# Gate matrices of two prompt tiles by indirect accumulating DMAs, and the output projection in the expert weight buffers

## The chip, the cores and the metric

One core of one Trainium2 chip runs the whole layer. The metric is device microseconds of that core, from launch to end; the median of three runs of the kernel before is 2303.07 us (2301.51 to 2303.24).

## What is computed

The reference is one hybrid encoder layer on two token sets with shared weights: 512 prompt tokens (tiles 0 to 3 of 128) and 256 sample tokens (tiles 4 and 5). Attention comes first; the change touches the output projection behind it and the PEER layer:

```python
x = x + jnp.concatenate([o_a, o_b], axis=-1) @ w_out[l]
x = x + peer(rms_norm(x, ffn_norm_g[l]), ...)

def peer(h, w_q, sub_keys, u, v):          # per chunk of 128 tokens
    q = (xc @ w_q).reshape(TOKEN_CHUNK, PEER_HEADS, 2, D_KEY_HALF)
    sc = einsum('cpzk,znk->cpzn', q, sub_keys)
    top_v, top_i = lax.top_k(sc, PEER_TOPK)
    cand = top_v[:, :, 0, :, None] + top_v[:, :, 1, None, :]
    best, pos = lax.top_k(cand, PEER_TOPK)
    eidx = take_along_axis(cand_idx, pos)   # i * 128 + j
    g = softmax(best)
    act = gelu(einsum('cd,cpkd->cpk', xc, u[eidx]))
    return einsum('cpk,cpkd->cd', g * act, v[eidx])
```

There are 128 x 128 experts (i, j). Each token picks 8 heads x 16 = 128 of them, each with a gate weight.

## The kernel before, in words

All matrix products in float32 are made of three products of a high and a low part (`mm3`, `split`). The work stands in this order:

- The sample tokens are normalized and projected by `w_in` (`in_project`, weights `wraw` by SyncE's DMA queue, three buffers); sample attention, the prompt's projection, prompt attention and the sample's output projection follow and overlap.
- The sample tiles are routed (`route_keys`, `route_pairs`); `eidx` holds their experts.
- The prompt's output projection (L534 to L561): `mixed` splits the mixed heads into `mh` and `ml`, the weights `wraw` come through a pool of its own (`wout`, three buffers of 128x512), then four norm-transposes make `x2p`.
- Prompt routing (`route_keys` with `prompt_weights`) with the first 16 steps of `hidden`. `hidden(j)` (L589) loads the 512 KB block `uT[j]` into `raw`, splits it, multiplies it by all 512 prompt tokens in PSUM tile `pu` (24 matmuls), applies GELU and stores `h_d`. `weights8` gives it three `raw` buffers and two each of `hi` and `lo`.
- The gate stage (L630 to L657). For each prompt tile `picked` takes the chosen pairs and gate weights. Then VectorE makes one-hot matrices `oij` and the gate-weighted `og`, four tokens at a time TensorE multiplies them into `pg` (12 matmuls of 128 columns), ScalarE copies `pg` into `gb`, and 16 DMAs store `gb` to `g_d`, a dense gate matrix [i, j, token]. The remaining 112 steps of `hidden` are interleaved with it.
- The value stage (L680 to L702): 64 pairs of j. Gates `gblk` come from `g_d` (one load for 8 values of j), `gw` is the pair's activations from `h_d`, VectorE multiplies them (L688), the product is split into `w`, the values `raw` into `hi` and `lo`, and TensorE adds 48 matmuls into the eight `py` banks.
- Beside the prompt, the 256 sample tokens are done sparsely: 256 indirect gathers (`row`, L725, 1 MB each, issued by GpSimd into four buffers), each followed by a dot product (L727) and an accumulation `acc` (L735) on VectorE.

What sets the order: each engine runs its instructions in the order in which a scheduler wrote them when the program was built; `tc.add_manual_dep` with `NOSYNC` ties a dot product to a step of `hidden` or of the value stage (`early`, `low_of`) in that order without a wait. Each queue of DMAs is issued in order by its engine: loads and most stores by SyncE, `h_d` and `g_d` by ScalarE, indirect ones by GpSimd.

Of the kernel before, what the change touches and what calls it, by code (L numbers as in the profile page):

```python
# [11 lines left out]
F32 = mybir.dt.float32  # L12
F32R = mybir.dt.float32r
# [31 lines left out]
NCAND = 64  # L45
FIRST_GATHER = 36
FILL = 16
NOSYNC = mybir.DependencyInfo(mybir.DependencyClass.NoSync, mybir.DependencyReason.DATA)


@with_exitstack
def tile_kernel(ctx, tc, xs_in, relb, onehot, logm, g1, w_in, gqk, lamv, gdiff, w_out, g2,
# [7 lines left out]
    def pool(stack, name, bufs=1, side="left", **kw):  # L60
        return stack.enter_context(tc.tile_pool(name=name, bufs=bufs, side=side, reuse_waits="tile", **kw))
# [38 lines left out]
    g_d = dram.tile([DENSE * P // TB, P, NK, TB], F32, name="g_d")  # L100


    ident = const.tile([P, P], F32, name="ident")
# [6 lines left out]
    def stage():  # L110
        return late.tile([P, D], F32, tag="st4", name="st4", bufs=3)
# [50 lines left out]

        project(lhs, n, w_in, 6, banks, evac, lows)

    def attention(n, pj, hrs, mix, order, psc, ptr):
        w = n * P
        turn, turn2 = itertools.count(), itertools.count()

# [181 lines left out]
    attention(2, pjS, hrS, mixS, ORDER, [ps_sc], [ps_tr])  # L350
# [190 lines left out]
    wo = pool(wox, "wo", DC)  # L541
    half = []
    for d in range(DC):
        raw = wpool.tile([P, 512], F32, name="wraw")
        nc.sync.dma_start(raw, w_out[d * P:(d + 1) * P, 512:])
        wh = wo.tile([P, 512], F32R, name="woh")
        wl = wo.tile([P, 512], F32R, name="wol")
        split(wh, wl, raw, G if d % 2 else V)
        half.append((wh, wl))
# [80 lines left out]
    nxt = picked(0)  # L630
    for t in range(DENSE):
        ijT, gp_ = nxt
        if t + 1 < DENSE:
            nxt = picked(t + 1)
        for tb in range(P // TB):
            gb = gm.tile([P, NK, TB], F32, name="gb")
            for tq in range(TB // TQ):
                c0 = tb * TB + tq * TQ
                oij = gm.tile([P, 2, TQ, NK], BF, name="oij")
                og = [gm.tile([P, TQ, NK], BF, name=f"og{k}") for k in range(3)]  # L640
                both = [P, 2 * TQ, NK // 2, 2]
# [15 lines left out]
            nc.scalar.dma_start(g_d[t * (P // TB) + tb], gb)  # L657
# [10 lines left out]
    vrows = uv.rearrange("(i j) d -> j i d", j=NK)  # L668

    def gates(jb):  # L670
        gblk = dp.tile([P, DENSE * P // TB, JB, TB], F32, name="gblk")
        nc.sync.dma_start(gblk, g_d[:, :, jb * JB:(jb + 1) * JB, :].rearrange("b i j t -> i b j t"))
        return gblk

    def values_of(j):
        vr, vh, vl = weights8(vrows[j, :, D:].rearrange("i (c d) -> i c d", d=P))
# [3 lines left out]
    for jp in range(NK // 2):  # L680
        jj = 2 * jp % JB
        wh, wl = (late.tile([P, 2, 2, 512], F32R, tag=f"x{i}", name=f"w{i}") for i in range(2)) if jp == 0 else (wh, wl)
        if jj == 0:
            gblk = gates(2 * jp // JB)
        ge = dp.tile([P, 2, 512], F32, name="gw", bufs=3)
        nc.sync.dma_start(ge, h_d[jp])
        ge4 = ge.rearrange("p k (b t) -> p k b t", t=TB)
        V.tensor_tensor(ge4, ge4, gblk[:, :, jj:jj + 2].rearrange("p b k t -> p k b t"), op=OP.mult)  # L688
        gh, gl = wh[:, jp % 2], wl[:, jp % 2]
        split(gh, gl, ge, V)  # L690
        vv = [values_of(2 * jp + k) for k in range(2)]
# [101 lines left out]
```

## Time and profile before

| what | value |
| --- | --- |
| median of 3 runs | 2303.07 us |
| profiled execution, its own time | 2314.86 us |
| its span, first to last instruction | 2313.0 us |
| granted TensorE clock, mean | 0.969 |
| TensorE busy | 93% of the span |
| VectorE busy | 77% |
| ScalarE busy | 40% |
| GpSimd busy | 36% |
| moved by DMA | 617.65 MB |

The profile is one execution. Busy time of TensorE counts pipelined matmuls, so a full engine can show less than 100%. A wait is put down to what came last. A stretch of the span is named by its start and end in us.

### The profile page before, as it was taken

Reading aid. Unit: us, or ns where it says so; the run is one execution under the profiler, and the core shown is the slowest. Engines: PE = TensorE matmul, PEld = TensorE weight load, DVE = VectorE, ACT = ScalarE, POOL = GpSimd, SP = SyncE. Lnnn points to the kernel's source line nnn. Section 1 sums busy time; section 2 is a strip of 40 time slices with the busy share of each in tenths; the row PEclk is TensorE's granted clock in tenths of the full one; section 3 lists DMA queues with packets and bytes.
Section 4 is the critical chain, followed back from the end, with each engine's and each line's share of the span. In section 5 each row is a group of like instructions: output and inputs, shape, how many; then the busy total and the mean of one; then the engine's idle time right before and its main releaser. Section 6 shows DMA issues by size and latency. Waiting matters only on the chain.

```text
span 2313.0 us, 31093 instructions
## 1 busy us (share of the span) xinstructions
PE 2159.4 (93%) x11312; PEld 1779.3 (77%) x11312; DVE 1791.0 (77%) x3500; ACT 915.4 (40%) x1484; POOL 835.9 (36%) x634
## 2 busy tenths in 40 slices
PE   7999999848899989999999996999999999999998
PEld 4788789836687867877888875887887887888776
DVE  4645379992589899989999974676887887887886
ACT  4765577621322324554555532222222222223232
POOL 4767766623456532222223231221222222221221
PEclk9999999958899999999999998999999999999999
DMA  5633333303577776888998999898999899999985
GB/s 183 184 109 125 104 120 94 114 19 102 196 248 269 262 263 220 289 302 316 344 349 341 347 363 343 307 351 302 346 360 374 326 366 357 370 362 349 375 341 190
DMA packets 198681, 617.65 MB, mean 267 GB/s; under 512 B 16016, under 2 KB 82192, under 8 KB 163712
## 3 DMA queue, kind: packets, MB, share of 16 engines
q1 hardware_dynamic: 139968, 278.70, 34.8%
q0 software_dynamic: 36864, 268.45, 30.7%
q10 hardware_dynamic: 21696, 68.53, 7.7%
q8 instruction: 88, 1.44, 0.2%
q14 instruction: 65, 0.53, 0.1%
HBM read 542.17 MB, written 73.45 MB: 266 GB/s over the span
## 4 chain that ended last, share of the span: by engine, by line
PE 64%; DMA 12%; DVE 10%; issue 8%; POOL 4%; ACT 2%; SPq 0%; ACTq 0%; POOLq 0%; DVEq 0%
PE py L67 8%; PE py L68 8%; PE py L69 8%; PE pu L67 6%; PE pu L69 6%; PE pu L68 6%; DMA raw<-in_uv_dram 4%; PE pacc L68 3%; DMA row<-in_uv_dram,eidx 3%; PE pacc L69 3%; PE pacc L67 3%; POOL row L725 2%; DMA wraw<-in_w_in_dram 2%; PE pg L653 2%; PE pq L69 2%
## 5 line engine op out<-in xcount | busy, mean ns | idle before, releaser
L725 POOL DMA_INDIRECT row<-in_uv_dram,eidx x256 | 399.0, 1559 | 1179.3 <-DVE acc L735 1041.8
L72 ACT CAST hi<-raw 128x1024 fp32r<-128x1024 f32 x272 | 285.1, 1052 | 594.2 <-PE pu L68 237.4
L67 PE MATMUL pu<-x2p,hi 128*128 128x512 f32 x1024 | 409.5, 400 | 18.5 <-ACT hi L72 18.5
L69 PE MATMUL pu<-x2p,lo 128*128 128x512 f32 x1024 | 408.6, 400 | 15.7 <-DVE lo L73 11.8
L67 PE MATMUL py<-w,hi 128*128 128x512 f32 x1024 | 400.9, 393 | 18.4 <-ACT hi L72 15.9
L68 PE MATMUL pu<-x2p,hi 128*128 128x512 f32 x1024 | 406.6, 397 | 0.0
L73 DVE TENSOR_TENSOR lo<-raw,hi 128x1024 fp32r<-128x1024 f32 x236 | 287.4, 1221 | 151.6 <-ACT hi L72 123.3
L68 PE MATMUL py<-w,hi 128*128 128x512 f32 x1024 | 400.4, 391 | 1.1 <-DVE w L73 1.1
L727 DVE CUSTOM_DVE_ANT_0 row<-row,st 128x1024 f32<-128x1024 f32 x256 | 332.2, 1305 | 64.0 <-DMA row<-in_uv_dram,eidx 63.9
L735 DVE SCALAR_TENSOR_TENSOR acc<-row,wgt,acc 128x1024 f32<-128x1024 f32 x256 | 328.2, 1282 | 5.3
L69 PE MATMUL py<-w,lo 128*128 128x512 f32 x1024 | 294.2, 389 | 0.4 <-DVE lo L73 0.4
L67 PEld LDWEIGHTS py<-w,hi 128*128 128x128 f32 x1024 | 193.2, 189 | 66.1 <-ACT hi L72 23.6
L67 PEld LDWEIGHTS pu<-x2p,hi 128*128 128x128 f32 x1024 | 195.5, 191 | 61.7 <-ACT hi L72 20.2
L69 PEld LDWEIGHTS pu<-x2p,lo 128*128 128x128 f32 x1024 | 194.9, 190 | 59.5 <-DVE lo L73 16.1
L68 PEld LDWEIGHTS py<-w,hi 128*128 128x128 f32 x1024 | 193.4, 189 | 41.4 <-DVE w L73 1.6
L68 PEld LDWEIGHTS pu<-x2p,hi 128*128 128x128 f32 x1024 | 195.0, 190 | 38.8
L69 PEld LDWEIGHTS py<-w,lo 128*128 128x128 f32 x1024 | 192.1, 188 | 40.7 <-DVE lo L73 0.8
L656 ACT COPY gb<-pg 128x512 f32<-128x512 f32 x128 | 132.5, 1142 | 82.1 <-PE pg L653 81.1
L73 POOL TENSOR_TENSOR wl<-wraw,wh 128x512 fp32r<-128x512 f32 x96 | 126.0, 1319 | 86.3 <-ACT wh L72 82.3
L72 ACT CAST w<-gw 128x1024 fp32r<-128x1024 f32 x64 | 67.0, 1049 | 168.4 <-PE py L69 167.7
L72 ACT CAST wh<-wraw 128x512 fp32r<-128x512 f32 x120 | 74.4, 623 | 104.0 <-DMA wraw<-in_w_in_dram 38.7
L732 ACT ACTIVATE wgt<-h 128x2 f32<-128x2 f32 x128 | 26.2, 205 | 224.8 <-DVE h L727 223.0
(303 smaller groups left out, 3700.5 us busy)
## 6 DMA issues: line engine op xcount, KB each, us to landing
raw<-in_uT_dram SPq DMA_DIRECT2D x128, 512.0 KB
raw<-in_uv_dram SPq DMA_DIRECT2D x128, 512.0 KB
h_d<-ge ACTq DMA_DIRECT2D x128, 256.0 KB
g_d<-gb ACTq DMA_DIRECT2D x16, 2048.0 KB
gblk<-g_d SPq DMA_DIRECT2D x16, 2048.0 KB
gw<-h_d SPq DMA_DIRECT2D x64, 512.0 KB
wraw<-in_w_in_dram SPq DMA_DIRECT2D x96, 256.0 KB
toe<-bias_d SPq DMA_DIRECT2D x24, 448.0 KB
```

The lines of the kernel that those rows point to most:

```text
L67: T.matmul(ps, ah, bh, start=start, stop=False)
L68: T.matmul(ps, ah, bl, start=False, stop=False)
L69: T.matmul(ps, al, bh, start=False, stop=stop)
L72: S.copy(hi, raw)
L73: return (low or G).tensor_tensor(lo, raw, f(hi), op=OP.subtract)
L653: T.matmul(pg[:, c], oij[:, 0, c4 * 4 + c], og[k][:, c4 * 4 + c], start=k == 0, stop=k == 2)
L656: S.copy(gb[:, :, o:o + 4].rearrange("p j t -> p t j"), pg)
L725: G.indirect_dma_start(out=r, out_offset=None, in_=uv, in_offset=bass.IndirectOffsetOnAxis(ap=eidx[t][:, b + k:b + k + 1], axis=0))
L727: dot = V.tensor_tensor_reduce(r[:, :D], r[:, :D], x2r[t], 1.0, 0.0, OP.mult, OP.add, h[:, k:k + 1])
L732: S.activation(wgt, h, AF.Gelu)
L735: V.scalar_tensor_tensor(acc, rows[k][:, D:], wgt[:, k:k + 1], acc, op0=OP.mult, op1=OP.add)
```

## The change

1. `SCAT = 2`: the gate matrices of prompt tiles 0 and 1 are no longer made by one-hot products. Two arrays `s_d` [i, j, token] of 8 MB each in DRAM are filled with zeros by 16 DMAs of 1 MB (`clear`, written into the sample attention, one pair behind each A head). For each tile the index `si` = (i * 128 + j) * 128 + token and the gate weight `gt` are made on VectorE, and 128 indirect DMAs per tile (`put`), each of 128 single floats, add the weights into `s_d`. `NOSYNC` ties put `k` to `hidden` step 24 + k * 92 / 256. Tiles 2 and 3 stay as they were; `g_d` halves.
2. The value stage loads `gs` from `s_d` beside a half-sized `gblk`, and multiplies `gw` in two halves.
3. The prompt's output projection loads `w_out` in blocks of 512 KB through `raw8`, `hi8` and `lo8` of the expert weights, and the pool `wout` is gone.

```diff
+    s_d = [dram.tile([P, NK, P], F32, name=f"s_d{t}") for t in range(SCAT)]
...
+    zero = stage()
+    V.memset(zero, 0.0)
+
+    def clear(kind, h):
+        if kind == 0:
+            for s_ in s_d:
+                nc.sync.dma_start(s_.rearrange("i j t -> i (j t)")[:, h * 2048:(h + 1) * 2048]
+                                  .rearrange("i (a n) -> i a n", n=D), zero[:, None].to_broadcast([P, 2, D]))
+
+    attention(2, pjS, hrS, mixS, ORDER, [ps_sc], [ps_tr], clear)
...
-    project((mh, ml), 4, w_out, 1, (obanks,), evac)
+    def out_weights(d, nb, hi, lo):
+        raw = wide(rw.tile([P, DC, P], F32, name="raw8", bufs=3))
+        nc.sync.dma_start(raw, w_out[d * P:(d + 2) * P, nb * 512:(nb + 1) * 512].rearrange("(k p) n -> p k n", p=P))
+        split(hi, lo, raw, G if d % 4 else V)
+        return hi, lo
...
+    for t in range(SCAT):
+        gt, si = (o[t][:, 0].rearrange("p k h -> p (k h)") for o in (tv, ti))
+        ei, ej = route_pairs(rq, t, gt)
...
+        V.tensor_scalar(i_, i_, float(P), tok, op0=OP.mult, op1=OP.add)
+        V.tensor_copy(si, i_)
+        scat.append((si, gt))
+    nxt = picked(SCAT)
+    for t in range(SCAT, DENSE):
...
+    for k in range(NPK * SCAT):
+        t, c = k % SCAT, k // SCAT
+        si, gt = scat[t]
+        put = G.indirect_dma_start(out=s_d[t].rearrange("i j (t one) -> (i j t) one", one=1),
+                                   out_offset=bass.IndirectOffsetOnAxis(ap=si[:, c:c + 1], axis=0),
+                                   in_=gt[:, c:c + 1], in_offset=None, compute_op=OP.add)
+        after = low_of[FIRST_SCATTER + k * (LAST_SCATTER - FIRST_SCATTER) // (NPK * SCAT)]
+        tc.add_manual_dep(put.ins, after.ins.name, NOSYNC, reason="order")
...
+        gs = dp.tile([P, SCAT, JB, P], F32, name="gs")
+        for t in range(SCAT):
+            nc.sync.dma_start(gs[:, t], s_d[t][:, jb * JB:(jb + 1) * JB])
```

How the built program orders it, at three places. A name in brackets is what the instruction waits for: `DMAHW` and `DMASW` are completions of DMAs issued by SyncE or ScalarE and by GpSimd, the others are engines. Line numbers of the changed kernel differ: its puts are L706, gathers L780, dot products L782, accumulations L790, splits L76, gate products L743.

First place, SyncE at the start, where the sample's weights are loaded. Before, from the sixth weight block on:

```order
L140 DMA wraw_228<-in_w_in_dram 128x512 [waits DMAHW2_49,Pool_49]
L346 DMA xin0_853<-in_xs_in_dram 128x1024 [waits DMAHW3_49]
L346 DMA xin0_853<-in_xs_in_dram 128x1024 [waits DMAHW4_49]
L140 DMA wraw_240<-in_w_in_dram 128x512 [waits DMAHW7_49,DMAHW6_49,DVE_49]
L217 DMA toe_949<-bias_d_96 128x896 [waits DMAHW6_49,DMAHW5_49,DMAHW0_49]
```

Now, with 12 more of the 16 zero fills between the two parts:

```order
L352 DMA xin0_855<-in_xs_in_dram 128x1024 [waits DMAHW4_49]
L362 DMA s_d0_104<-st4_947 128x2x1024 [waits DMAHW5_49,DVE_49]
L362 DMA s_d1_105<-st4_947 128x2x1024 [waits DMAHW6_49]
...
L362 DMA s_d0_104<-st4_947 128x2x1024 [waits DMAHW5_49]
L362 DMA s_d1_105<-st4_947 128x2x1024 [waits DMAHW6_49]
L144 DMA wraw_242<-in_w_in_dram 128x512 [waits DMAHW7_49,DVE_49]
```

All 16 fills have moved ahead of the seventh weight block, and stand in one piece.

Second place, the end of the `hidden` steps, on VectorE. Here `lo8_13957` belongs to the last step (j = 127), `lo8_14283` and `lo8_14289` to the first two values. Before, the first gate products stand some 25 steps earlier:

```order
L73 TENSOR_TENSOR lo8_14271<-raw8_14268,hi8_14270 128x1024 [waits DMAHW4_49,PE_49,Activation_49]
L727 ISA row_20184,h_20182<-row_20184,st4_5144 128x1024 [waits DMASW4_49]
L727 ISA h_20182 128x1
L73 TENSOR_TENSOR lo8_14305<-raw8_14302,hi8_14304 128x1024 [waits DMAHW6_49,PE_49,Activation_49]
L733 TENSOR_TENSOR wgt_20183<-wgt_20183,gate4_5200 128x2 [waits Activation_49]
L735 SCALAR_TENSOR_TENSOR acc_19532<-row_20184,wgt_20183,acc_19532 128x1024 [waits DVE_49]
L735 SCALAR_TENSOR_TENSOR acc_19532<-row_20187,wgt_20183,acc_19532 128x1024 [waits DVE_49]
L688 TENSOR_TENSOR gw_15281<-gw_15281,gblk_15279 128x1024 [waits DMAHW7_49,DMAHW1_49,DMAHW0_49]
```

Now:

```order
L76 TENSOR_TENSOR lo8_13957<-raw8_13954,hi8_13956 128x1024 [waits DMAHW5_49,PE_49,Activation_49]
L782 ISA row_19460,h_19455<-row_19460,st4_5186 128x1024 [waits DMASW2_49]
L782 ISA h_19455 128x1
L76 TENSOR_TENSOR lo8_14283<-raw8_14280,hi8_14282 128x1024 [waits DMAHW7_49,PE_49,Activation_49]
L76 TENSOR_TENSOR lo8_14289<-raw8_14286,hi8_14288 128x1024 [waits DMAHW1_49,PE_49,Activation_49]
...
L790 SCALAR_TENSOR_TENSOR acc_19405<-row_19457,wgt_19456,acc_19405 128x1024 [waits DVE_49]
L790 SCALAR_TENSOR_TENSOR acc_19405<-row_19460,wgt_19456,acc_19405 128x1024 [waits DVE_49]
L743 TENSOR_TENSOR gw_14274<-gw_14274,gs_14269 128x2x256 [waits DMAHW3_49,DMAHW1_49,DMAHW0_49]
```

The first gate product has moved behind the last `hidden` step. On GpSimd the puts stand at the same place like this (before, GpSimd had gathers alone there):

```order
L706 DMA s_d0_104<-tv0_6808,ti0_6809 2097152x1 [waits DMASW7_49,DMASW1_49]
L706 DMA s_d1_105<-tv1_6810,ti1_6811 2097152x1 [waits DMASW2_49,DMASW0_49]
L780 DMA row_19481<-in_uv_dram,eidx5_5219 128x2048 [waits DVE_49]
L780 DMA row_19484<-in_uv_dram,eidx5_5219 128x2048 [waits DVE_49]
L706 DMA s_d0_104<-tv0_6808,ti0_6809 2097152x1 [waits DMASW5_49,DMASW1_49]
L706 DMA s_d1_105<-tv1_6810,ti1_6811 2097152x1 [waits DMASW6_49,DMASW2_49]
L706 DMA s_d0_104<-tv0_6808,ti0_6809 2097152x1 [waits DMASW5_49]
L706 DMA s_d1_105<-tv1_6810,ti1_6811 2097152x1 [waits DMASW6_49]
```

135 puts stand ahead of gathers 141 and 142 (`row_19481`, `row_19484`), and 121 behind them without a gather between: 55 pairs, then 11 of tile 1 alone. Each put waits for the completion of the put before it on the same tile, and the first load of `gs` for the completion of the last put of both tiles.

Third place, SyncE ahead of the prompt's output projection. Before, five expert loads go first, then `w_out`:

```order
L575 DMA raw8_6861<-in_w_q_dram 128x8x128
L575 DMA raw8_6895<-in_uT_dram 128x1024 [waits DMAHW4_49]
L575 DMA raw8_6930<-in_w_q_dram 128x8x128 [waits DMAHW5_49]
L575 DMA raw8_7003<-in_uT_dram 128x1024 [waits DMAHW6_49,DMAHW3_49,Pool_49]
L575 DMA raw8_7038<-in_w_q_dram 128x8x128 [waits DMAHW7_49,DMAHW4_49,Pool_49]
L140 DMA wraw_6437<-in_w_out_dram 128x512 [waits DMAHW0_49,DVE_49]
```

Now:

```order
L559 DMA raw8_6456<-in_w_out_dram 128x2x512
L559 DMA raw8_6486<-in_w_out_dram 128x2x512 [waits DMAHW4_49,DVE_49,PE_49]
L559 DMA raw8_6516<-in_w_out_dram 128x2x512 [waits DMAHW5_49,DVE_49,PE_49]
L559 DMA raw8_6546<-in_w_out_dram 128x2x512 [waits DMAHW6_49,DMAHW3_49,DVE_49]
L559 DMA raw8_6583<-in_w_out_dram 128x2x512 [waits DMAHW7_49,DMAHW4_49,Pool_49]
```

`w_out` has moved ahead of the expert loads and takes their buffers. On VectorE its first split (`lo8_6455`) stands right behind the cast to `eidx4`, where before the routing of tile 5 ran to its end first.

## Rows read from the trace of the kernel before

**Rows 1.** The page: span, and busy time of the engines.

```profile
span 2313.0 us, 31093 instructions
PE 2159.4 (93%) x11312; PEld 1779.3 (77%) x11312; DVE 1791.0 (77%) x3500; ACT 915.4 (40%) x1484; POOL 835.9 (36%) x634
```

**Rows 2.** Windows by stage: engines' busy us (instructions), granted clock, DMA share, GB/s.

```profile
500.00:526.00 26.00, 1.12 (x4) 0.72 (x4) 25.34 (x75) 3.51 (x5) 4.97 (x2) 0.50 0.13 40
820.00:1377.00 557.00, 540.60 (x3551) 439.18 (x3549) 519.18 (x925) 269.14 (x350) 146.25 (x89) 0.99 0.85 314
1377.00:1400.00 23.00, 12.54 (x50) 9.56 (x51) 7.97 (x10) 4.93 (x7) 3.82 (x2) 0.82 1.04 400
1400.00:1574.00 174.00, 163.69 (x694) 133.21 (x692) 109.32 (x132) 48.65 (x74) 40.31 (x28) 0.96 0.87 328
1574.00:2303.00 729.00, 711.35 (x3132) 583.57 (x3133) 585.26 (x670) 203.25 (x252) 174.19 (x116) 1.00 0.91 343
```

**Rows 3.** Tiles `pu` and `py`: matmuls, ns min/median/max, first and last start.

```profile
L69 PE MATMUL pu<-x2p,lo x1024: 387/389/796, 598.5 to 1571.4; 128*128 128x512 f32 x171
L67 PE MATMUL py<-w,hi x1024: 387/389/796, 1574.1 to 2303.4; 128*128 128x512 f32 x171
```

**Rows 4.** DMA view of the first 100 us: GB/s in 40 slices of 2.5 us.

```profile
GB/s 38 344 356 260 73 239 231 362 326 5 34 86 313 340 34 226 78 211 114 116 199 173 57 233 163 178 147 132 183 217 290 161 98 214 206 30 221 252 225 115
```

**Rows 5.** Chain that ended last, 29 to 50 us: start, us, what.

```profile
29.61 5.23 DMA wraw<-in_w_in_dram
...
35.60 1.69 PE pacc L67 x4
...
41.71 3.75 DMA wraw<-in_w_in_dram
...
47.24 2.59 DMA wraw<-in_w_in_dram
```

**Rows 6.** Timeline around the prompt's output projection, DVE and PE: start, us, instruction, [idle before].

```profile
510.75 0.21 DVE L528 CAST eidx<-ijf 128x128 uint32<-128x128 f32 x1
...
526.15 1.48 DVE L525 TENSOR_TENSOR ej<-ej 128x1024 bf16<-128x1024 bf16 x3
...
529.76 2.08 PE L67 MATMUL pacc<-wh,mh 128*128 128x512 f32 x4 [26.66 <-ACT wh L72]
```

**Rows 7.** Groups of the gate stage, by shape: busy us, mean ns, idle before.

```profile
L642 DVE TENSOR_TENSOR oij<-ijT,iotaj 128x2048 bf16<-128x2048 bf16 x64 | 77.6, 1217 | 1.3 <-PE pg L653 1.3
L646 DVE TENSOR_TENSOR og<-oij,gp__9559 128x1024 bf16<-128x1024 bf16 x48 | 30.2, 684 | 0.0
L615 PE MATMUL pt<-identb,ei 128*128 128x128 bf16 x64 | 4.6, 220 | 0.6 <-DVE ei L494 0.6
```

**Rows 8.** Chain in the gate stage: twelve-matmul groups of `pg`, two at a time.

```profile
1131.20 1.36 PE pg L653 x24
```

**Rows 9.** Waits within 1377 to 1400 us: who, for whom, us, times, longest.

```profile
PEld pu L67 <- ACT hi L72: 10.8, 1, 10.8
```

**Rows 10.** Timeline of GpSimd, first gathers, VectorE nearly idle.

```profile
577.47 0.94 POOL L725 DMA_INDIRECT row<-in_uv_dram,eidx  x1 [0.30 <-PE pacc L69]
578.71 0.94 POOL L725 DMA_INDIRECT row<-in_uv_dram,eidx  x1 [0.30 <-issue]
```

**Rows 11.** Chain at the end: stores of 256 KB on otherwise idle queues.

```profile
2301.25 2.26 DMA out_dram<-yo
...
2307.24 2.01 DMA out_dram<-yo
```

**Rows 12.** Tile `row` on GpSimd: gathers, issue ns min/median/max; and one landing, from the chain.

```profile
L725 POOL DMA_INDIRECT row<-in_uv_dram,eidx x256: 933/1677/5496, 575.9 to 2270.1; - x128
...
1359.22 15.23 DMA row<-in_uv_dram,eidx
```

**Rows 13.** GpSimd within 820 to 1377 us, costliest group.

```profile
L725 POOL DMA_INDIRECT row<-in_uv_dram,eidx x76 | 135.3, 1780 | 400.7 <-DVE acc L735 325.5 <-DVE pos L461 15.5 <-DVE c L459 14.1
```

More of the change, by code (lines that the diff above doesn't have):

```diff
@@ L47 @@
 FILL = 16
+SCAT = 2
+FIRST_SCATTER = 24
+LAST_SCATTER = 116
 NOSYNC = mybir.DependencyInfo(mybir.DependencyClass.NoSync, mybir.DependencyReason.DATA)
@@ L99, in tile_kernel @@
     x1_d = [dram.tile([P, D], F32, name=f"x1_d{t}") for t in range(NT)]
-    g_d = dram.tile([DENSE * P // TB, P, NK, TB], F32, name="g_d")
+    g_d = dram.tile([(DENSE - SCAT) * P // TB, P, NK, TB], F32, name="g_d")
+    s_d = [dram.tile([P, NK, P], F32, name=f"s_d{t}") for t in range(SCAT)]
     ident = const.tile([P, P], F32, name="ident")
@@ L163, in in_project, with attention @@
         project(lhs, n, w_in, 6, banks, evac, lows)
-    def attention(n, pj, hrs, mix, order, psc, ptr):
+    def attention(n, pj, hrs, mix, order, psc, ptr, fill=None):
         w = n * P
@@ L277, in attention @@
             (head_a if kind == 0 else head_b)(h)
+            if fill is not None:
+                fill(kind, h)
     def mixed(n, mix, pp):
@@ L534, in tile_kernel @@
     rw = pool(ctx, "rw", 2)
-    wpool = pool(right, "wout", 3, side="right")
     mh, ml = mixed(4, mixP, ppP)
@@ L538, in tile_kernel, with wide @@
     obanks = (ps_sc, ps_sc2, ps_tr, ps_tr2)
-    project((mh, ml), 4, w_out, 1, (obanks,), evac)
+    def wide(t):
+        return t.rearrange("p (k a) n -> p k (a n)", k=2)
+    def out_weights(d, nb, hi, lo):
[3 more added lines that the diff above has]
+        return hi, lo
+    ps = [bank(b, "pacc") for b in obanks]
+    for d in range(0, DC, 2):
+        wh, wl = out_weights(d, 0, *(wide(rw.tile([P, DC, P], F32R, name=k)) for k in ("hi8", "lo8")))
+        for t in range(4):
+            cs = slice(t * P, (t + 1) * P)
+            for k in range(2):
+                mm3(ps[t], mh[:, d + k, cs], ml[:, d + k, cs], wh[:, k], wl[:, k], d + k == 0, d + k == DC - 1)
+    for t in range(4):
+        evac(t, 0, ps[t])
     wox = ctx.enter_context(ExitStack())
-    wo = pool(wox, "wo", DC)
+    wo = pool(wox, "wo", DC // 2)
     half = []
[L543 to L549, printed above, removed]
+    for d in range(0, DC, 2):
+        wh, wl = out_weights(d, 1, *(wo.tile([P, 2, 512], F32R, name=k) for k in ("woh", "wol")))
+        half += [(wh[:, k], wl[:, k]) for k in range(2)]
     x2p = [late.tile([P, DC, 512], F32R, tag=f"x{i}", name=f"x2p{i}") for i in range(2)]
@@ L628, in picked @@
         return ijT, gp_
-    nxt = picked(0)
-    for t in range(DENSE):
+    tok = gm.tile([P, 1], F32, name="tok", bufs=1)
+    G.iota(tok, pattern=[[0, 1]], base=0, channel_multiplier=1, allow_small_or_imprecise_dtypes=True)
+    scat = []
+    for t in range(SCAT):
+        gt, si = (o[t][:, 0].rearrange("p k h -> p (k h)") for o in (tv, ti))
+        ei, ej = route_pairs(rq, t, gt)
+        for m in (8, 4, 2):
+            V.tensor_tensor(ej[:, :m], ej[:, :m], ej[:, m:2 * m], op=OP.add)
+        i_, j_ = (rq.tile([P, NPK], F32, name="n1_") for _ in range(2))
+        V.tensor_reduce(i_, ei.rearrange("p m r -> p r m"), axis=AX.X, op=OP.add)
+        V.tensor_tensor(j_, ej[:, 0], ej[:, 1], op=OP.add)
+        V.scalar_tensor_tensor(i_, i_, float(NK), j_, op0=OP.mult, op1=OP.add)
+        V.tensor_scalar(i_, i_, float(P), tok, op0=OP.mult, op1=OP.add)
[3 more added lines that the diff above has]
+    for t in range(SCAT, DENSE):
         ijT, gp_ = nxt
@@ L656, in tile_kernel @@
                     S.copy(gb[:, :, o:o + 4].rearrange("p j t -> p t j"), pg)
-            nc.scalar.dma_start(g_d[t * (P // TB) + tb], gb)
+            nc.scalar.dma_start(g_d[(t - SCAT) * (P // TB) + tb], gb)
     for j in range(FILL, NK):
         hidden(j, G if j < 20 else V)
+    for k in range(NPK * SCAT):
[6 more added lines that the diff above has]
+        tc.add_manual_dep(put.ins, after.ins.name, NOSYNC, reason="order")
     left.close()
@@ L670, in gates @@
     def gates(jb):
-        gblk = dp.tile([P, DENSE * P // TB, JB, TB], F32, name="gblk")
+        gs = dp.tile([P, SCAT, JB, P], F32, name="gs")
+        for t in range(SCAT):
+            nc.sync.dma_start(gs[:, t], s_d[t][:, jb * JB:(jb + 1) * JB])
+        gblk = dp.tile([P, (DENSE - SCAT) * P // TB, JB, TB], F32, name="gblk")
         nc.sync.dma_start(gblk, g_d[:, :, jb * JB:(jb + 1) * JB, :].rearrange("b i j t -> i b j t"))
-        return gblk
+        return gs, gblk
     def values_of(j):
@@ L683, in tile_kernel @@
         if jj == 0:
-            gblk = gates(2 * jp // JB)
+            gs, gblk = gates(2 * jp // JB)
         ge = dp.tile([P, 2, 512], F32, name="gw", bufs=3)
         nc.sync.dma_start(ge, h_d[jp])
-        ge4 = ge.rearrange("p k (b t) -> p k b t", t=TB)
-        V.tensor_tensor(ge4, ge4, gblk[:, :, jj:jj + 2].rearrange("p b k t -> p k b t"), op=OP.mult)
+        for ge4, g4 in ((ge[:, :, :SCAT * P].rearrange("p k (b t) -> p k b t", t=P), gs),
+                        (ge[:, :, SCAT * P:].rearrange("p k (b t) -> p k b t", t=TB), gblk)):
+            V.tensor_tensor(ge4, ge4, g4[:, :, jj:jj + 2].rearrange("p b k t -> p k b t"), op=OP.mult)
         gh, gl = wh[:, jp % 2], wl[:, jp % 2]
```

1 line of the change is left out of this document (removed).

## The prediction

> **What bounds the kernel now.** I read the page first, for the span and the busy shares [rows 1]: TensorE works 2159.4 of 2313.0 us, VectorE 77%, GpSimd 36%. A share is a mean over stages, so next come the windows [rows 2], cut at the first and last matmuls of `pu` and `py` [rows 3]. There the reader sees TensorE full in the gate stage (540.6 of 557 us), in the last hidden steps (163.7 of 174) and in the values (711.4 of 729), and two holes: 500 to 526 us (1.1 of 26) and 1377 to 1400 us (12.5 of 23, with the DMA engines at 1.04 and 400 GB/s, the clock at 0.82). So TensorE's own instructions, and whatever keeps TensorE waiting, set the end. What the other engines do counts only where TensorE waits for it. The chain of waits for the start [rows 5] and the timeline of the hole at 500 us [rows 6] then tell what those waits are, and the orders above tell which of them the change moves. The sum is made against the profiled execution's own 2314.86 us; the median shown is 11.8 us lower, and that is taken off at the end.
>
> **A. The zero fills: +39.** 16 DMAs of 1 MB, 16.8 MB, now stand on SyncE's queue in one piece behind the `xin` loads and ahead of the seventh weight block. Before, the `xin` loads end at about 22.5 us (the rate falls from 326 to 5 GB/s there, [rows 4]), and that block lands at 34.84 us (29.61 + 5.23); TensorE's `pacc` follows at 35.60 [rows 5]. TensorE takes its matmuls in order and has nothing else to do. At the 343 GB/s of a well-filled stage [rows 2], 16.8 MB take 49 us; the block then needs 2.59 us of its own [rows 5] and lands at 22.5 + 49 + 2.6 = 74.1, 39 us late. Bounds: at 400 GB/s [rows 2] +32; at the whole run's mean of 267 GB/s (617.65 MB in 2313 us) +53. Later weight blocks shift with it and add nothing.
>
> **B. The output projection: -17.** `w_out` waits no longer for the routing of tile 5: its loads stand ahead of the expert loads, and its first split right behind the cast to `eidx4`. Before, that cast ends at 510.96 us and TensorE starts at 529.76 after 26.66 us idle, VectorE still working at `ej` at 526.15 [rows 6]. Now the split takes some 1.2 us and TensorE can start at about 512.2, 17.5 us earlier. Bounds: 0, if the routing pushed back is waited for next; -22 if nothing of the hole but 4 us is left. Its matmuls are as many as before.
>
> **C. The gates of tiles 0 and 1: -47.** Half of the gate products go: 64 groups of 12 matmuls, 768 at 1.36/24 = 0.0567 us [rows 8], 43.5 us; with 64 transposes of `pt`, priced at the same 0.0567 since pipelined, 3.6 us. TensorE being full there, all of this counts. Bounds: -40, and -63 if the transposes cost their own 220 ns [rows 7] and some waits go too. On VectorE 32 `oij` of 1.217 and 96 `og` of 0.684 us go [rows 7], 104.6 us; the index arithmetic and the second half of each gate product come in, which TensorE covers: VectorE has 38 us free in the gate window even before [rows 2], and 144 us in the value stage, against some 64 added instructions of about 0.15 us each, an estimate of 9 us. Were that cover gone, those 9 us would be the price.
>
> **D. The burst of gate loads: -11.** Before, the first gate products stand among the hidden steps, and their loads make the hole at 1377, where TensorE's weight loads wait 10.8 us for `hi` [rows 9]. Now they come behind the last step. Bounds: 0 to -20.
>
> **E. Puts among the gathers: +25.** 135 of the 256 puts stand on GpSimd ahead of gathers 141 and 142. Each waits for the put before on its tile, and behind it wait the gathers, then the dot products that stand between VectorE's splits. GpSimd had 325.5 us in which it only waited for `acc` within 557 us [rows 13], so 67 steps of 4 us (268, priced under F) fit, but beside 1 MB gathers that land in 15.23 us under load [rows 12] some will be late. Bounds: 0, if all fits, and 110, if each pair costs 1.6 us more of TensorE's time. I take 25, near the low end, since the gathers have four buffers.
>
> **F. The border between hidden steps and values: +278.** This is the term that decides. Gathers 141 and 142 wait for the two `acc` of gathers 137 and 138. On VectorE these stand behind `lo8` of the second value, and that waits for TensorE's matmuls of the last hidden step, since `hi8` and `lo8` have two buffers each. GpSimd takes its queue in order, so the remaining 121 puts begin only when TensorE has nothing hidden left to do. Its next work, `py`, needs `gw` times `gs`, and the first load of `gs` waits for the last put of both tiles. So the tail of 55 pairs and 11 single puts, 66 steps in each tile's chain, lies open. One step is an issue of 0.94, a gap of 0.30 [rows 10], a write of which the receipt is waited for, 2.26 [rows 11], and, since adding must first read the destination, some more. Bounds: 3.50 without any reading and 5.76 with a second 2.26; I take 4.0, near the low end, since the stores of rows 11 move 256 KB and a put 512 bytes. 66 x 4.0 = 264. Ahead of it stand some 6 us of VectorE's dot products and `acc`; behind it 1 MB of `gs`, 1 MB of `gblk` and a `gw` of 0.5 MB at 343 GB/s, multiplied and split, 10 us. The gap between last `pu` and first `py` before, 1571.4 + 0.4 to 1574.1, some 2.3 us [rows 3], goes. 6 + 264 + 10 - 2 = 278. The bounds of the tail alone are 121 issues at 1.24, 150 us, if receipts hold nothing up, and 66 x 5.76, 380.
>
> The Trainium skill, "DMA: Bandwidth & Descriptors", section "Anatomy of one DMA — SWDGE (gpsimd) path", gives a fixed cost of about 2.0 us per DMA, most of it the receipt for the last write. By that figure the step would be 3.24 us, the tail an estimated 214 and the median some 2520; no trace here shows an adding DMA.
>
> **The sum.** 39 - 17 - 47 - 11 + 25 + 278 = +267: 2581.9 for the profiled execution, **2570** for the median. All lower ends together (+32, -22, -63, -20, 0, +164) give +91 and 2394; all upper ones (+53, 0, -40, 0, +110, +394) +517 and 2820.
>
> **The rivals.** *The tail is limited by issue alone.* If GpSimd can run ahead of receipts, as it does between gathers [rows 10], 264 becomes 150: 2456. For it: a gather's issue is short; against it: each put names the completion of the one before. Chance 0.20.
>
> *The tail or the hidden stage is slower.* With 5.76 us a step, 380 instead of 264: 2686. Or the puts among the gathers cost their upper bound, 85 more: 2655. GpSimd's issues are 0.933 us at best, 1.677 in the median and 5.496 at worst [rows 12], longer where VectorE is busy. If all 135 early puts took the longest, they and 96 gathers at 1.68 would need 742 + 161 = 903 us of some 690 between the first put and the last hidden step, 213 too many in place of the 25: 2758. Together 0.20, 0.05 of it for the last.
>
> The Trainium skill, "SBUF — State Buffer", section "A bandwidth-pool intuition that's wrong (but worth ruling out)", says that a DMA issued by GpSimd that takes about 620 ns alone takes about 3100 beside a VectorE copy, because it cannot write its descriptors: a factor of 5, so an estimated 4.7 us a put. The trace agrees in direction, with 0.93 and 1.68; its longest is near that factor, its median far from it.
>
> *The other side: the tail is nearly free.* All terms without the 264 sum to about +3; with the hidden stage unhurt (E at 0) they are -22. So 66 steps would have to cost under 22 us, 0.33 each, for the change to gain; at 0.2 each the time is 2303 - 22 + 13 = 2294. That is the case if GpSimd gets the last puts done beside the hidden steps after all, because the gathers' wait for `acc` clears early. For it: GpSimd is 36% busy [rows 1]. Against it: the wait on the last hidden step is in the order, and an issue alone is 0.94 + 0.30 [rows 10]. Chance 0.03. That the change doesn't act, or that gains and losses cancel: 0.02, at 2303.
>
> If the zero fills were hidden after all, 39 us go and the time is 2531, inside the main case.
>
> **How the numbers follow.** The main case, a waited-for tail with steps of 3.2 to 4.8 us (211 to 317) and the other terms spread between their bounds, covers 2470 to 2660 and has 0.55. The range of 2420 to 2750 adds most of the issue-limited tail and most of the slow cases; left out are the gaining and unchanged cases (0.05), the lower fringe of the first rival and the upper fringe of the second, some 0.15 to 0.2 together. Some 4.6 us, 0.2%, can be told from no change here. Faster 0.03, same 0.02, slower 0.95.
>
> **What would show it.** A: TensorE's pause from about 36 to 75 us, ended by a `wraw` load, with a stretch near 343 GB/s before it. B: the first `pacc` of the output projection at about 512 us plus the shift of A, and the wait for `wh` ahead of it under 10 us. C: `pg` with half its matmuls. D: no DMA share above 1 within the hidden steps. E: dot products waiting for `row` between puts. F: a hole of 250 to 300 us between the last `pu` and the first `py`, TensorE idle, GpSimd issuing puts in pairs every 4 us, ended by a load of `gs`. I am wrong if the first `py` follows the last `pu` within 100 us, if the puts of the hole come every 1.2 us or less, or if the hidden stage grows by over 100 us.

## The result, and the profile after

The changed kernel takes 2551.09 us (median of 4 runs, 2542.61 to 2557.9) against 2302.29 for the kernel before (4 runs, 2297.38 to 2303.24): ratio 1.1081, 95% interval 1.1056 to 1.1105, so 249 us slower. The prediction was 2570, +267. Its profiled execution took 2557.90 us.

The page of the kernel after: span, busy time, and TensorE, GpSimd and clock in 40 slices.

```profile
span 2556.1 us, 29558 instructions
PE 2116.8 (83%) x10478; PEld 1742.6 (68%) x10478; DVE 1722.9 (67%) x3449; ACT 849.9 (33%) x1404; POOL 1267.1 (50%) x883
...
PE   3999999868999987799999993000399999999998
...
POOL 1677865522655247767565566887222222222221
PEclk7999999869999998999999997555699999999999
```

Against [rows 1] TensorE is busy 43 us less and the span is 243 us longer. Nearly all of that is the three zeros in TensorE's line, and below them GpSimd has some of its fullest slices. Tiles `pu` and `py` give the edges. Beside [rows 3], these are the first weight load of `pu` and the last matmul of `py` before:

```profile
L67 PEld LDWEIGHTS pu<-x2p,hi x1024: 186/188/338, 593.9 to 1570.7; 128*128 128x128 f32 x171
...
L69 PE MATMUL py<-w,lo x1024: 387/389/504, 1577.7 to 2303.8; 128*128 128x512 f32 x171
```

And after:

```profile
L70 PE MATMUL pu<-x2p,hi x1024: 386/389/629, 612.1 to 1558.1; 128*128 128x512 f32 x171
...
L72 PE MATMUL pu<-x2p,lo x1024: 387/389/797, 615.8 to 1558.6; 128*128 128x512 f32 x171
```

```profile
L70 PE MATMUL py<-w,hi x1024: 387/389/797, 1830.1 to 2546.1; 128*128 128x512 f32 x171
...
L72 PE MATMUL py<-w,lo x1024: 388/389/629, 1834.1 to 2546.5; 128*128 128x512 f32 x171
```

Cut there, the difference of the two spans is (a stage ends with its last matmul's start and 0.4 us):

| stage | before, us | after, us | difference | predicted |
| --- | --- | --- | --- | --- |
| to the first `pu` | 593.9 | 612.1 | +18.2 | +22 (A and B) |
| hidden steps and gates | 977.9 | 946.9 | -31.0 | -33 (C, D, E) |
| last `pu` to first `py` | 2.3 | 271.1 | +268.8 | +278 (F) |
| values | 730.1 | 716.8 | -13.3 | 0 |
| end | 8.8 | 9.2 | +0.4 | 0 |
| sum | 2313.0 | 2556.1 | +243.1 | +267 |

Windows of the kernel after, by these stages (columns as in [rows 2]):

```profile
612.00:1559.00 947.00, 886.63 (x4483) 721.53 (x4482) 738.31 (x1595) 321.55 (x459) 560.55 (x322) 0.97 0.83 284
1559.00:1830.00 271.00, 0.00 (x0) 0.00 (x0) 8.46 (x12) 2.51 (x4) 194.78 (x125) 0.51 0.27 29
1830.00:2547.00 717.00, 710.53 (x3136) 584.20 (x3136) 586.35 (x728) 203.85 (x251) 173.75 (x114) 1.00 0.92 350
```

In the hole TensorE does nothing and its granted clock stands at 0.51, the lower of its two levels; the DMA engines move 29 GB/s, and GpSimd is busy 195 of 271 us. The timeline of GpSimd over the start of the hole (columns as in [rows 10]):

```profile
1563.15 1.65 POOL L706 DMA_INDIRECT s_d<-tv,ti  x1 [6.03 <-DMA s_d<-tv,ti]
1565.10 2.42 POOL L706 DMA_INDIRECT s_d<-tv,ti  x1 [0.30 <-issue]
1567.83 1.00 POOL L780 DMA_INDIRECT row<-in_uv_dram,eidx  x1 [0.30 <-issue]
1569.13 0.97 POOL L780 DMA_INDIRECT row<-in_uv_dram,eidx  x1 [0.30 <-issue]
1570.41 1.62 POOL L706 DMA_INDIRECT s_d<-tv,ti  x1 [0.30 <-issue]
1572.33 1.58 POOL L706 DMA_INDIRECT s_d<-tv,ti  x1 [0.30 <-issue]
1577.45 1.56 POOL L706 DMA_INDIRECT s_d<-tv,ti  x1 [3.54 <-DMA s_d<-tv,ti]
1579.32 1.56 POOL L706 DMA_INDIRECT s_d<-tv,ti  x1 [0.30 <-issue]
```

Gathers 141 and 142 stand at 1567.8 and 1569.1, and the 121 puts begin at 1570.4, 11 us after the last hidden matmul, as the order said. The two `acc` that the prediction has them wait for end at 1566.1; the puts ahead of them, of which the first waited 6.03 us for a landing, held the gathers a little longer than that. But from 1577.45 on the puts come every 1.86 us and wait for nothing: 1.56 of issue and a gap of 0.30. Only the 11 single puts of tile 1 at the end wait for a completion. The chain of waits, which in the kernel after goes through the hole:

```profile
1811.91 3.04 DMA s_d<-tv,ti
1814.95 0.27 issue
1815.22 3.12 DMA s_d<-tv,ti
1818.35 0.33 SPq L724
...
1819.20 8.38 DMA gw<-h_d
1827.70 1.30 DVE gw L743 x2
```

A put lands 3.0 to 3.1 us after its issue began, the next follows 0.27 later, and the last one releases the load of `gs` on SyncE, behind which `gw` is loaded. So the tail is 55 pairs of 2 x 1.86 and 11 singles of 3.3 us, 205 + 36 = 241; with a wait of 3.5 behind the first pair, and some 3 us more, mostly one longer wait where the pairs end, it lasts 248 us, from 1570.4 to 1818.3.

At the start, the DMA view of the first 100 us (2.5 us a slice, as [rows 4]) and the chain (as [rows 5]):

```profile
GB/s 41 336 359 256 78 225 279 324 377 422 421 419 424 421 421 419 423 419 419 421 419 423 423 418 350 326 364 247 121 61 171 150 113 205 137 78 205 159 180 164
```

```profile
23.32 17.37 DMA s_d<-st
...
48.40 15.92 DMA wraw<-in_w_in_dram
64.42 0.63 ACT wh L75
```

The fills run at 420 GB/s from about 22 to 60 us, and the block behind them lands at 64.3 (48.40 + 15.92) instead of 34.84: 29.5 us late.

The timeline of TensorE around the output projection of the kernel after (to set against [rows 6]):

```profile
536.46 2.07 PE L70 MATMUL pacc<-hi,mh 128*128 128x512 f32 x4 [2.37 <-ACT hi L75]
541.25 0.80 PE L71 MATMUL pacc<-lo,mh 128*128 128x512 f32 x1 [2.72 <-DVE lo L76]
...
570.76 0.79 PE L70 MATMUL pacc<-woh,mh 128*128 128x512 f32 x1 [4.94 <-DVE x L299]
```

The second half of the projection (`woh`) began like this before:

```profile
554.45 0.50 PE L67 MATMUL pacc<-woh,mh 128*128 128x512 f32 x1 [0.29 <-DVE x L293]
```

The idle 26.66 us are gone. With A's 29.5 taken off, the projection starts at 507, 23 us early. But between its start and the first `pu` there are now 75.6 us (612.1 - 536.5) instead of 64.1: 11.5 are given back. About 8 of them are waits for VectorE, which now does tile 5's routing in between: 2.72, 0.92 (at 555.3) and 4.94, against 0.29 before. Some 2 more come with the last of these waits: over the second half the granted clock is 0.90 in the mean (570.7 to 596 us), where it was 1.00 before (554.4 to 577.2).

### The profile page after: what moved, and what is told of

Same layout as the page of the kernel before. It is cut to its first block, busy times and chain, and to the rows that moved or that the text cites. A ratio compares the mean times of both kernels' runs of the same rounds, so it can differ in the third digit from the quotient of the medians.

```text
span 2556.1 us, 29558 instructions
## 1 busy us (share of the span) xinstructions
PE 2116.8 (83%) x10478; PEld 1742.6 (68%) x10478; DVE 1722.9 (67%) x3449; ACT 849.9 (33%) x1404; POOL 1267.1 (50%) x883
## 4 chain that ended last, share of the span: by engine, by line
PE 51%; DMA 16%; POOL 14%; DVE 9%; issue 7%; ACT 2%; SPq 0%; ACTq 0%; POOLq 0%; DVEq 0%
POOL s_d L706 10%; PE py L70 8%; PE py L71 7%; DMA s_d<-tv,ti 7%; PE py L72 7%; PE pu L70 4%; PE pu L72 4%; PE pu L71 4%; DMA raw<-in_uv_dram 3%; DMA row<-in_uv_dram,eidx 3%; PE pacc L71 3%; PE pacc L72 3%; PE pacc L70 2%; POOL row L780 2%; PE pq L72 2%
## 5 line engine op out<-in xcount | busy, mean ns | idle before, releaser
L780 POOL DMA_INDIRECT row<-in_uv_dram,eidx x256 | 382.9, 1496 | 776.1 <-DVE acc L790 650.8
L70 PE MATMUL py<-w,hi 128*128 128x512 f32 x1024 | 401.0, 394 | 277.4 <-ACT w L75 271.1
L706 POOL DMA_INDIRECT s_d<-tv,ti x256 | 457.3, 1786 | 191.4 <-DMA s_d<-tv,ti 129.3
L782 DVE CUSTOM_DVE_ANT_0 row<-row,st 128x1024 f32<-128x1024 f32 x256 | 330.8, 1302 | 98.3 <-DMA row<-in_uv_dram,eidx 98.3
L76 DVE TENSOR_TENSOR lo<-raw,hi 128x1024 fp32r<-128x1024 f32 x238 | 290.1, 1220 | 150.5 <-ACT hi L75 123.9
L790 DVE SCALAR_TENSOR_TENSOR acc<-row,wgt,acc 128x1024 f32<-128x1024 f32 x256 | 328.1, 1282 | 5.5
L743 DVE TENSOR_TENSOR gw<-gw,gs 128x512 f32<-128x512 f32 x64 | 43.9, 685 | 272.1 <-DMA gw<-h_d 272.1
L76 POOL TENSOR_TENSOR wl<-wraw,wh 128x512 fp32r<-128x512 f32 x88 | 114.7, 1309 | 81.0 <-ACT wh L75 80.6
```

Source lines behind the costliest of these rows:

```text
L70: T.matmul(ps, ah, bh, start=start, stop=False)
L706: put = G.indirect_dma_start(out=s_d[t].rearrange("i j (t one) -> (i j t) one", one=1), out_offset=bass.IndirectOffsetOnAxis(ap=si[:, c:c ...
L743: V.tensor_tensor(ge4, ge4, g4[:, :, jj:jj + 2].rearrange("p b k t -> p k b t"), op=OP.mult)
L780: G.indirect_dma_start(out=r, out_offset=None, in_=uv, in_offset=bass.IndirectOffsetOnAxis(ap=eidx[t][:, b + k:b + k + 1], axis=0))
L782: dot = V.tensor_tensor_reduce(r[:, :D], r[:, :D], x2r[t], 1.0, 0.0, OP.mult, OP.add, h[:, k:k + 1])
L790: V.scalar_tensor_tensor(acc, rows[k][:, D:], wgt[:, k:k + 1], acc, op0=OP.mult, op1=OP.add)
```

## The experiments

All times are medians of the runs, with the kernel before run beside them on the same chip (2299 to 2303 there). Stages are read from one profile each, and one execution differs from another by some 10 us (the profiled one of before is 11.8 above its median), so differences of that size between stages are not read as effects.

**The puts left out** (`e1_no_puts`).

```diff
-    for k in range(NPK * SCAT):
-        ...
-        put = G.indirect_dma_start(out=s_d[t]...)
```

> The 256 puts are left out and nothing else (zero fills, loads of gs and products stay, so the weights of tiles 0 and 1 are missing from the gates). Theory, puts behind the last hidden step lie open: the hole of 271 us between the last pu and the first py goes but for some 2 to 12 us, and the hidden stage loses a few us of waits for lo, so 2551 - 260 to 285: 2266 to 2291 us. Rival, the border is held by the late loads of gs, gblk and gw themselves: still over 2500. Rival, the puts also cost TensorE much within the hidden stage (the upper bound of 110 in the prediction): under 2200.

2276.96 us (2266.62 to 2282.28), ratio to before 0.9868 (0.9811 to 0.9924). Its tiles:

```profile
L72 PE MATMUL pu<-x2p,lo x1024: 387/389/797, 616.9 to 1550.9; 128*128 128x512 f32 x171
```

```profile
L70 PE MATMUL py<-w,hi x1024: 387/389/632, 1553.6 to 2270.1; 128*128 128x512 f32 x171
```

The hole is 2.3 us, and 274 us are gone, within the theory's range. The late loads at the border were not what held it. The hidden stage takes 938 us against 947, but this cannot be read as the price of the puts in it: without them TensorE's matmuls stand in another order there. What is left of the change without its puts is 25 us faster than before.

**Fills tied behind their heads, and fills spread out** (`e2_late_fills`, `e5_spread_fills`).

```diff
+                tc.add_manual_dep(z.ins, tail[0].ins.name, NOSYNC, reason="order")
```

Here `tail[0]` is the copy at the end of an A head: of the sample's attention in the first run; in the second of the prompt's, with 15 of the 16 fills as `nc.sync.dma_start(s_, parts[0])` from the first megabyte.

> Each pair of zero fills is tied behind the A head it belongs to, so the fills no longer stand ahead of the seventh weight block. Theory, the fills cost what that block comes late (64.4 against 34.8 us in the profiles): 30 us less, 2521 us, first pu at about 582 us instead of 612, hole at the border unchanged at about 271. Rival, the fills cost the same wherever they stand since the weight loads share the DMA engines: 0 to 10 us less, 2541 to 2551.

> One fill of 1 MB comes from VectorE's zeros as before, the other 15 copy it within DRAM, two behind each A head of the prompt's attention, where the DMA engines move only some 100 GB/s. Theory, the 15 us that the late fills of the run before still cost (first pu at 596.2 against 581.6 us with the projection alone) come from 12 of 16 fills crowded into 100 to 150 us beside the weight loads: now the first pu comes at 582 to 585, the hole at the border stays 271, 2521 us. Rival, 16.8 MB cost 15 us wherever they stand: 2536.

The first: 2538.35 us (2538.15 to 2544.11), 13 less, not 30. Its first `pu` is at 596.2, 16 us earlier than after. The projection alone (below) has it at 581.6, so 14.6 us remain. The window from 100 to 150 us shows about half of them:

```profile
100.00:150.00 50.00, 42.38 (x217) 31.72 (x218) 32.73 (x96) 32.60 (x88) 23.58 (x30) 0.90 0.93 363
```

TensorE loses 7.6 of 50 us there, with the DMA engines at 0.93; before it had 49.74 of them. The second: 2509.27 (2502.28 to 2522.95), 42 less than after, with the hole as it was (1508.4 to 1779.1). Its fills lie between 294.5 and 395 us, and the first `pu` is at 571.7. So the fills' cost goes when they stand where the DMA engines are free. 15 of them also come from DRAM now and no longer from VectorE's tile; the run before, which moved them alone, gained 16 us at the first `pu`, and beyond that place and source were not parted. The gain is 10 us more than the theory gives; the first `pu` is even earlier than with the projection alone (581.6). The tie also reorders the prompt's attention, and what of the 10 us is due to that was not tried.

**The output projection alone** (`e3_projection_alone`, and `e10_projection_again` beside the last runs). The third part of the change put on the kernel before.

> The kernel before with the third part alone (output projection in the expert weight buffers). Theory: the projection starts some 18 to 23 us earlier, but in the profile after it gives back part of that while it runs; the first pu came 12 us earlier than the fills alone would make it. 2303 - 12: 2291 us, from 2285 to 2297. Rival, the routing that is pushed back is waited for afterwards: 2303 within 3.

> The kernel before with the output projection in the expert buffers alone, once more beside the run above: 2291 to 2297 by the first measurement, 2294. If the run above is not below this one, the puts earn nothing and the third part of the change is all that is worth keeping.

2293.97 us, ratio 0.9950 (0.9922 to 0.9977), then 2291.42, ratio 0.9959 (0.9944 to 0.9973): 8 to 10 us faster than before, within the theory's range. The timeline of TensorE in the second of them:

```profile
506.02 2.07 PE L67 MATMUL pacc<-hi,mh 128*128 128x512 f32 x4 [2.37 <-ACT hi L72]
...
540.26 0.79 PE L67 MATMUL pacc<-woh,mh 128*128 128x512 f32 x1 [5.08 <-DVE x L293]
```

It starts 23.7 us before [rows 6] and its first `pu`, at 581.8, is 12.1 earlier. Half is given back on the way, as in the full change.

**Puts that write instead of adding** (`e4_plain_puts`): `compute_op=OP.add` removed.

> The puts write instead of adding (where two heads of a token pick the same expert, one weight is lost). Theory A, adding is what lengthens an issue from a gather's 0.94 to a put's 1.56 us: issues of 0.94, pairs every 2.5 to 3.1 us instead of 3.73, tail 40 to 65 us shorter, about 2490 to 2510. Theory B, the many single-float destinations do it: issues stay at 1.56 and the tail at 253, 2551 within 10. Either way the landing of a put beside nothing else (3.0 us) falls only if reading the destination is part of it.

2453.05 us (one run), 98 less than after: theory A, and more than it said. The timeline of GpSimd in the pairs and in the singles:

```profile
1562.18 0.97 POOL L706 DMA_INDIRECT s_d<-tv,ti  x1 [0.30 <-issue]
1563.46 0.97 POOL L706 DMA_INDIRECT s_d<-tv,ti  x1 [0.30 <-issue]
```

```profile
1711.42 0.97 POOL L706 DMA_INDIRECT s_d<-tv,ti  x1 [1.44 <-DMA s_d<-tv,ti]
1713.82 0.97 POOL L706 DMA_INDIRECT s_d<-tv,ti  x1 [1.42 <-DMA s_d<-tv,ti]
```

An issue takes 0.97 us, near a gather's 0.94, and a pair 2 x 1.275; a single put lands in 2.1 (2.40 less the 0.27 seen above) instead of 3.0. So adding costs 0.59 us of GpSimd and 0.9 us of landing in each put.

Of the shorter time, 75 us lie in the hole (196 instead of 271). The hidden stage is shorter too:

```profile
L72 PE MATMUL pu<-x2p,lo x1024: 387/389/792, 615.9 to 1531.7; 128*128 128x512 f32 x171
```

The first `pu` stands at 612.1 as after, so it takes 920 us, 27 less, with TensorE's matmuls in the very order of the kernel after. Against the three runs of two tiles in two chains with adding puts (937 to 947) it is 17 to 27 less. TensorE's waits there for `lo` and `og` fall from 51 to 30 us. So adding is paid for in the hidden stage as well, and not in the tail alone.

The Trainium skill, "DMA: Bandwidth & Descriptors", section "Anatomy of one DMA — SWDGE (gpsimd) path", has about 2.0 us fixed for a DMA that GpSimd issues: the plain put agrees with its 2.1, the adding one does not with its 3.0.

**More chains, and all puts of one tile first** (`e7_four_chains`, `e8_tile_by_tile`).

```diff
         t, c = k % SCAT, k // SCAT
+        s_ = s_d[t * 2 + c % 2]
...
-        put = G.indirect_dma_start(out=s_d[t].rearrange("i j (t one) -> (i j t) one", one=1),
+        put = G.indirect_dma_start(out=s_.rearrange("i j (t one) -> (i j t) one", one=1),
```

The value stage of this run loads one of the two arrays of each tile. The other run has `t, c = k // NPK, k % NPK` in the place of the first line, and nothing else changed.

> Two arrays for each tile, puts taking turns among four, so each waits for the fourth put before it; the value stage reads one of each tile's two arrays (half of the weights of tiles 0 and 1 are left out); 32 zero fills instead of 16. In the built order 25 puts stand in the tail instead of 121. Theory, the hole is what the order leaves behind the last hidden step: 25 x 1.86 + 20 = 66 us instead of 271; GpSimd gets 96 more puts, 180 us, into a hidden stage in which it had 192 us of waiting, so that grows by 0 to 60; fills + 40: 2551 - 205 + 30 + 40 = 2416, from 2380 to 2450. Rival, puts beside gathers cost the full 1.86 us of TensorE's time too: hidden stage 180 longer, 2566.

> All puts of tile 0, then all of tile 1, instead of taking turns: one chain at a time. In the built order 97 puts of tile 1 stand in the tail. Theory, a step is the longer of the issues in it and of issue, landing and gap of one put (3.3 us for the last 11 puts in the profile after): 97 x 3.3 = 320 and 20, hole of 340 us, 2551 + 70 = 2620. Rival, a step costs issue alone, 1.86: hole of 200, 2480. Rival, the prediction's step of 4.0 us for a put and its receipt: hole of 408, 2690.

Four chains: 2447.49 us (one run), hole of 73 us, hidden stage 991 us, 44 longer than after. The hole goes where the order has no puts, and part comes back as work beside the gathers: the time and the longer hidden stage lie in the theory's range, the hole is 7 us over its 66. Tile by tile: 2649.88 us (one run), hole of 357. The expectation miscounted here: rows of the order that repeat stand for several puts, and 143 puts stand in that tail, the first 98 still in two chains. By its own theory they cost 49 x 3.73 + 45 x 3.3 = 331; with 26 us around them that is the 357.

**Puts for one tile** (`e6_one_tile`, `e9_one_tile_two_arrays`, `e11_second_array_unread`, `e12_sum_left_out`).

```diff
-SCAT = 2
+SCAT = 1
...
+        V.tensor_tensor(gs[:, 0], gs[:, 0], gs[:, 1], op=OP.add)
+        gs = gs[:, :1]
```

The sum is in the run with two arrays (`e9_one_tile_two_arrays`) alone; all four have spread fills.

> Puts for tile 0 alone (128 in one chain; tiles 1 to 3 by one-hot products), spread fills. In the built order all 128 puts now stand ahead of the last 114 gathers, two gathers after each put. Theory, what costs is the tail behind the last hidden step: without it 2303 - 12 (projection) - 24 (half of the removed gate products) + 10 (last put, gs and gw loads at the border) + 5: 2282 us, from 2265 to 2300. Rival, a put under load lands after 7 us or more, and 128 in a chain need 900 us of the 650 that are left of the hidden stage: hole of up to 250 us again or a longer hidden stage, 2400 to 2550.

> As the run with one tile, but its puts take turns between two arrays, which VectorE adds up once for 8 values of j, so two chains run side by side. In the built order all 128 puts now stand ahead of gather 141, none in the tail (with one chain 45 stood there, hole 175). Theory, the tail is the whole of the loss: first pu at 570, hidden stage 960 to 970, hole under 20, values 715 to 725: 2265 to 2285 us, faster than the kernel before. Rival, puts beside gathers, and the second array's 8 MB of loads and sum, cost what the products gave: 2290 to 2310.

> As the run with one tile and two arrays, but the value stage loads and uses only the first array (half of tile 0's weights are left out), with no sum. There the values took 752 us, against 714 with one array. Theory, the second array's 8 MB of loads or its sums on VectorE make TensorE wait for hi: values 714 to 722, 2275 to 2285. Rival, it is what the long hole gave the other runs (loads made early): values 740 to 752 again, 2305 to 2316.

> As the run with one tile and two arrays, both loaded, but not added up (half of tile 0's weights are left out). Theory A, the loads are what costs: values 740 to 752. Theory B, the 16 sums of 1.2 us on VectorE and what they wait for: values 714 to 725.

One array: 2444.81 us (2429.0 to 2447.03), hole of 175 us. The same miscount: 45 puts of the one chain stand behind the last hidden step, not none. The time lies in the rival's range, but its reason, landings of 7 us or more, is not what the tail shows. Tile `s_d` on GpSimd from 1545 to 1690 us of this run:

```profile
L712 POOL DMA_INDIRECT s_d<-tv,ti x44: 1557/1559/1588, 1545.2 to 1686.7; - x44
...
  DMA s_d<-tv,ti: 79.4, 44
...
DMA to landing us min/median/max: 2.9/3.0/3.1
```

Each of the 44 waits for the one before. 45 x 3.3 = 149, and 26 around them. Two arrays: no put in the tail and a hole of 13.8 us, as the theory said, yet 2316.75 us, ratio 1.0068 (1.0043 to 1.0093): slower than before, and above the ranges of both the theory and the rival. The tiles and TensorE's waits of that run:

```profile
L70 PE MATMUL py<-w,hi x1024: 387/389/796, 1551.9 to 2304.2; 128*128 128x512 f32 x171
```

```profile
PE py L70 <- ACT hi L75: 30.5, 16, 8.9
```

The values take 753 us, and TensorE waits 30.5 us for `hi`. Without the second array they take 719 (2290.53 us in one run), with its loads but without the sum 758 (2322.81 in one run). So 8 MB more of loads in a stage whose DMA engines are 0.92 busy cost the 39 us, and the sums nothing that shows: theory A of the last expectation.

Over six kernels the hole is what the built order leaves behind the last hidden step, priced by one rule, a pair at twice the issue and gap, a single put at its landing and 0.3:

| run | puts behind | priced | hole | rest |
| --- | --- | --- | --- | --- |
| after | 55 pairs, 11 singles | 241 | 271 | 30 |
| plain puts | 55 pairs, 11 singles | 55 x 2.55 + 11 x 2.4 = 167 | 196 | 29 |
| tile by tile | 49 pairs, 45 singles | 331 | 357 | 26 |
| one tile | 45 singles | 149 | 175 | 26 |
| four chains | 25 in turns | 25 x 1.86 = 47 | 73 | 26 |
| two arrays | 0 | 0 | 14 | 14 |

In the kernel after, the rest of 30 is 11 us ahead of the tail, 12 behind it, and 7 of the longer waits in it.

No kernel here with puts and all its weights beats the one before. The output projection alone does: 2291.42 us.

## Why the prediction was right, and where its steps were off

**F, the border, +278, measured +268.8.** The mechanism is shown: the puts behind gathers 141 and 142, begun only after the last hidden step, with TensorE idle until `gs` is there; without puts the hole is gone. The step inside it failed. The prediction put a step of each tile's chain as an issue of 0.94, a gap of 0.30, a write of which the receipt is waited for, 2.26, and some more for reading: 4.0 us for each pair. In the pairs GpSimd doesn't wait for receipts: landing counts from the start of the issue (3.0, not 0.94 + 0.30 + 2.26 + reading) and hides under the other tile's put. The pair lasts 3.73 us since an adding put costs GpSimd 1.56 and not 0.94. So the mechanism inside the tail is that of the first rival, issue alone, at a higher price: 121 x 1.86 = 225 and 16 for the waits of the 11 singles, not 121 x 1.24 = 150. The 264 came near 248 by luck, because one error made up for the other.

**A, the zero fills, +39.** Mis-sized: 29.5 at the landing. 16.8 MB went at 420 GB/s, above the 343 taken and the upper bound of 400. **B, -17.** At the start of the projection it was 23, more than forecast; half of it was lost again to the routing that was pushed back, which the bound of 0 named and the value did not. Left are 12 us at the first `pu`, 8 to 10 in the medians.

**C, D, E: -47, -11, +25, measured -31 together.** The sum is right; how it divides is not settled. D shows by itself: TensorE's waits for `hi` in the hidden stage fall from 18.5 us (13 with the projection alone) to 1.2. E: with adding puts the stage takes 947, 941 and 937 us (after, late fills, spread fills), without puts 938, but in another order of matmuls, and with plain puts in the same order 920. So the run without puts prices them at 0 to 9 us and the run with plain puts, for the adding alone, at 17 to 27; the forecast 25 is borne out by the second and not by the first. C and D hang on the same choice. The stage takes 978 us before and 966 to 967 with the projection alone; the profile before is 11.8 above its median, so the second is the better base. From there the run without puts gives 29, the one with plain puts at least 47, of the forecast 58. Without puts TensorE still waits 25.3 us for `lo`, against 11.8 before. The matmuls themselves cost what rows 8 said, 2.47 us for 44 in the chain after, 56 ns each.

**The values, -13, were not in the sum.** The gates of tiles 0 and 1 come in 4 KB pieces where `g_d` has 1 KB: TensorE's waits in that stage, before and after:

```profile
PE py L67 <- ACT hi L72: 15.9, 14, 5.2
```

```profile
PE py L70 <- ACT hi L75: 6.2, 12, 1.4
```

All kernels with a smaller `g_d` and one array loaded for each tile take 712 to 721 us for the values, those with the whole one 730 to 737. The hole is not the reason, as the run without puts has none and takes 717. That fits fewer small pieces on busy DMA engines, and the two runs on the second array show how this stage answers to loads; the piece size alone was not tried.

**The rivals.** Issue alone: see F. A slower tail or hidden stage did not come: from 906 to 1559 us a put's issue takes 1.99 us in the mean and 5.27 at most, against 1.56 alone. The Trainium skill, "SBUF — State Buffer", section "A bandwidth-pool intuition that's wrong (but worth ruling out)", has some 620 ns for a DMA issued by GpSimd alone and some 3100 beside a VectorE copy, five times as long; here the longest issue is 3.4 times the 1.56, the mean 1.3 times. A nearly free tail was excluded by the order, as argued.

## What to carry to other kernels

A chain of DMAs in which each waits for the one before cost, in each step here, the longer of two things: the issues that stand between two links, and one landing. Count, in the built order, how many links stand behind the last work that could hide them, since engines take their queues in order and a single wait ahead of the chain can expose all of it. Removing matmuls from a full TensorE paid here only in the run without the puts that replaced them: the replacing work has to stand where its engine is free, zero fills and extra loads included. And a run that leaves work out prices that work only if the rest keeps its order.

## What the runs showed of the hardware

An indirect DMA of 128 single floats that adds took GpSimd 1.56 us to issue and landed in 3.0 us; one that only writes took 0.97 and 2.1. Beside 1 MB gathers on the same queue the adding put landed in 6.9 us in the median and 16.2 at most:

```profile
L706 POOL DMA_INDIRECT s_d<-tv,ti x133: 1552/1917/5267, 906.3 to 1554.6; - x133
...
DMA to landing us min/median/max: 3.0/6.9/16.2
```

That is the tile `s_d` on GpSimd from 906 to 1559 us of the kernel after. What these landings cost the hidden stage is part of E, and open as it is. Zero fills from a broadcast tile of VectorE reached 420 GB/s, more than any stage of the kernel before.
